# The third product of the mixers' output projection in whole float32, in a decoder block on one Trainium2 core

## The chip, the cores and the metric

The kernel runs on one core of a Trainium2 chip. The metric is the device time of one execution in microseconds; the median of the runs is quoted. Engines are named as in the profile: PE is TensorE's matmuls and PEld its weight loads, DVE is VectorE, ACT is ScalarE, POOL is GpSimd, SP is SyncE. SP and POOL issue most of the transfers from memory (DMAs).

## The reference

One decoder layer on 512 tokens of 1024 channels, with 256 memory tokens, all in float32. Three branches (a gated short convolution, a Conformer convolution, attention into the memory tokens) are weighted by gates and added; the sum goes through the output projection `w_o` (1024 x 1024), and the result is added to the residual rows. A gated feed-forward part and a norm follow.

```python
merged = g[:, :, 0] * y_a + g[:, :, 1] * y_b + g[:, :, 2] * y_c
x = x + merged @ w_o                                  # the product in question
h = _rmsnorm(x, norm_ffn_g)                           # needs every row of x
u = _causal_dwconv(h @ w_up, conv_ffn_w)
gt, up = jnp.split(u, 2, axis=-1)
x = x + (jax.nn.silu(gt) * up) @ w_down
return _rmsnorm(x, norm_final_g)
```

## The kernel before

**Products in parts.** PE multiplies in a reduced float32 form (`float32r`, fp32r in the profile). To keep the accuracy, each operand is split into a high part, a cast to that form, which ACT makes (`whi` or `whoh` of a weight, `mgh` of the merged activations), and a low part, the rest, which DVE makes (`wlo` or `whol`, `mgl`). One product is then three matmuls: high by high, high by low, low by high (`product`, L429 to L431). For some weights the low part is made by a DMA that adds the weight to the negated high part (L499, on POOL's queue).

**Seven products for eight.** A large product is cut into 2 x 2 blocks and worked out as seven block products by sums and differences of blocks (Strassen's scheme). In the output projection they are called a, b, f, c, d, e, g, in this order (`WO = "abfcdeg"`); f is the third. Each has an activation operand of 128 x 1024 (the blocks `m00`, `m01`, `m10`, `m11`, tiles `mg`, changed in place by L435 and L1627 between the products), a weight operand in two halves (tiles `wo`, sums of blocks of `w_o` made by DVE in L778 or by adding DMAs on POOL's queue in L1602 and L1609) and results of 2 x 128 x 512 in PSUM (`bank`). So each has 8 steps of 3 matmuls. f's weight is the tile `("wo", "x", i)`; c's and d's come from `("wo", "y", i)`, to which DVE adds f's weight for c and a POOL DMA adds another block for g; e has its own. DVE adds the results to the four row blocks of the residual, `x` (L1704).

**After the projection** ACT squares each row block (L1711) and takes the root (L1717), DVE scales it (L1722, `xnorm`), PE transposes it (L1730), and the products with `w_up` begin. The transposes of the first two row blocks stand ahead of each half of product g.

**The order of the work.** Nothing is issued when it is defined: `Jobs` collects all steps with an engine, a planned cost, what they need and which buffers they take. PE's steps keep the order in which they are written; for each other engine `Jobs.run` places the next step by planned start and due time, and gives out the buffers (the rings `sb` and `lf` in SBUF, `ps` in PSUM). Every engine and every DMA queue then works strictly in that order, so an instruction that waits holds up all behind it. The split weights take turns in four buffers, in the order of `the_unit`; six weight halves of the projection have buffers of their own (`WO_HELD`).

The casts of merged activations are written in L1644, their low parts in L1649; casts of weights in L478, their low parts in L482. ACT's cast of e's two weight halves needs the adding DMAs of L1602 to have landed.

Of the kernel before, what the change touches and what calls it, by code (L numbers as in the profile page):

```python
# [14 lines left out]
P = 128  # L15
# [39 lines left out]
HALF = SEQ // 2  # L55
LOAD_BUFS = 6
SHIFT = 192
SOON = 8.0

SHARE = 0.39  # L60
# [254 lines left out]
def hybrid_block_kernel(  # L315
# [19 lines left out]
    nc = tc.nc  # L335
# [29 lines left out]
    tiles = {}  # L365
# [14 lines left out]
    def two(key):  # L380

        return tiles[key].rearrange("p (c n) -> p c n", c=2)

    def four(key):
        return tiles[key].rearrange("p (k n) -> p k n", k=4)
# [14 lines left out]

    TAP = 0.665
    MM, MM_HALF, MM_QUAD = 0.2268, 0.12, 0.1142
    LOAD, MORE, MORE_WIDE = 1.42, 2.55, 2.55
    LOAD_LATENCY, MORE_LATENCY = 3.1, 3.4

# [36 lines left out]
    def pe(key, cost, fn, after=(), take=(), use=(), unit=True):  # L442
        pe_jobs[key] = (cost, fn, after, take, use)
        seq.append(key)
        if unit:
            the_unit(key, key)
# [8 lines left out]
    def split_job(unit, key, n_k, n, after, wide=None, lo_from=None, held=None):  # L455

        n_all = n_k * n

        def src():
            return wide() if wide is not None else tiles[key][:, :n_all]

        parts = []

        def high():
            if held:
                parts.extend(
                    forms.tile([P, 4, HALF], F32R, tag=held + s, name=name("who" + s)).rearrange(
                        "p k n -> p (k n)") for s in "hl"  # L470
                )
            else:
                parts.extend(
                    wts.tile([P, 1024], F32R, tag=s, name=name(s))[:, :n_all]
                    for s in ("whi", "wlo")
                )
            w_units[unit] = [t.rearrange("p (k n) -> p k n", k=n_k) for t in parts]
            nc.scalar.copy(parts[0], src())  # L478

        def low():  # L480
            hi, lo = parts
            nc.vector.tensor_tensor(lo, src(), hi.bitcast(F32), op=ALU.subtract)  # L482

        use = [key] if wide is None else []

        def define():
            if held:
                last = next(f for f in OPERAND if OPERAND[f] == held)
                before = [(("mq", 1), last)]
            else:  # L490
                i = unit_at[unit] - UNIT_BUFS
                before = [unit_uses[i][1]] if i >= 0 else []
            job(("wh", unit), "ACT", actv(n_all), high, list(after) + before, use=use)
            if lo_from is None:
                job(("wl", unit), "DVE", dve(n_all), low, [("wh", unit)], use=use)
            else:
                job(("wn", unit), "ACT", actv(n_all), lambda: nc.scalar.activation(
                    parts[1], src(), AF.Copy, scale=-1.0), [("wh", unit)], use=use)
                job(("wl", unit), "POOL", MORE, lambda: nc.gpsimd.dma_start(  # L499
                    out=parts[1], in_=lo_from, accum_op=ALU.add), [("wn", unit)],  # L500
                    MORE_LATENCY)

        deferred.append(define)
# [1079 lines left out]
    WO_SRC = {"a": (w_o[0, 0], w_o[0, 1]), "b": (w_o[0, 2], w_o[0, 3]), "d": (w_o[1, 2], w_o[1, 3])}  # L1583
    WO_LOWS = [(p, i) for p in "ab" for i in range(2)]

    def wo_bank(p):


        return "a" if p in "aceg" else "f" if p == "d" else p
# [4 lines left out]
    for i in range(2):  # L1594
        for key, src, take in (
            ("a", w_o[0, i], "wf"), ("b", w_o[0, 2 + i], "wf"), ("y", w_o[1, 2 + i], "lf"),
            ("x", w_o[0, i], "lf"), ("e", w_o[1, 2 + i], "sb"),
        ):
            after = {"y": late_rows, "x": late_rows, "e": [("wo", "a", 1)]}.get(key, ())
            fetch_job(("wo", key, i), src, after=after, take=(take,))  # L1600
        for key in "xe":
            job(("wadd", key, i), "POOL", MORE, lambda key=key, i=i: nc.gpsimd.dma_start(  # L1602
                out=tiles["wo", key, i], in_=w_o[1, i], accum_op=ALU.add),
                [("ld", ("wo", key, i))], MORE_LATENCY, use=[("wo", key, i)])
        deferred.append(lambda i=i: job(
            ("wsum", i), "DVE", dve(1024), lambda: add_into(("wo", "y", i), ("wo", "x", i)),
            [("wadd", "x", i), ("wl", ("wo", "d", i))], use=[("wo", "x", i), ("wo", "y", i)]))
        deferred.append(lambda i=i: job(
            ("wadd", "y", i), "POOL", MORE, lambda: nc.gpsimd.dma_start(  # L1609
                out=tiles["wo", "y", i], in_=w_o[0, 2 + i], accum_op=ALU.add),  # L1610
            [("wl", ("wo", "c", i))], MORE_LATENCY, use=[("wo", "y", i)]))
        for p, key, after in (
            ("a", "a", ("ld", ("wo", "a", i))), ("b", "b", ("ld", ("wo", "b", i))),
            ("d", "y", ("ld", ("wo", "y", i))), ("c", "y", ("wsum", i)),
            ("f", "x", ("wadd", "x", i)), ("e", "e", ("wadd", "e", i)),
            ("g", "y", ("wadd", "y", i)),
        ):
            split_job(("wo", p, i), ("wo", key, i), 2, 512, [after], held=WO_HELD.get((p, i)),
                      lo_from=WO_SRC[p][i] if (p, i) in WO_LOWS else None)

# [14 lines left out]
    def split_merged(n, p, at, halved, after):  # L1635
        src, hi, lo = SPLIT_FROM[p], ("mgh", p), ("mgl", p)
        first = not at.start
        end = (at.start // 512,) if halved else ()
        old = [hi + (0,)] if not first else []

        def high():
            if first:
                make(hi, F32R)
            nc.scalar.copy(tiles[hi][:, at], tiles[src][:, at])  # L1644

        def low():
            if first:
                make(lo, F32R)
            nc.vector.tensor_tensor(  # L1649
                tiles[lo][:, at], tiles[src][:, at], tiles[hi][:, at].bitcast(F32),  # L1650
                op=ALU.subtract
            )

        size = at.stop - at.start
        job(hi + end, "ACT", actv(size), high,
            after + old + ([wo_end(WO[n - 3])] if n > 2 else []),
            take=[(hi, "sb")] if first else [], use=[src] + ([] if first else [hi]))
        job(lo + end, "DVE", dve(size), low, [hi + end] + ([lo + (0,)] if not first else []),
            take=[(lo, "sb")] if first else [], use=[src, hi] + ([] if first else [lo]))

    for n, p in enumerate(WO):
        if p in "ab":
            m = 0 if p == "a" else 2
            for i in range(2):
                split_merged(n, p, slice(512 * i, 512 * (i + 1)), True, [("sum", 1, m + i, 0)])
        else:
            split_merged(n, p, slice(0, 1024), False,
                         [("sum", 1, 3, 1)] if p == "g" else [("ms", p)])

    def wo_lows(p, i):  # L1670
        return ("mgl", p, i) if p in "ab" else ("mgl", p)

    def wo_product(p, i, ts):
        w_hi, w_lo = w_units[("wo", p, i)]
        for k in (2 * i, 2 * i + 1):
            for t in ts:
                bank = ("bank", "wo", wo_bank(p), t)
                ps = make(bank) if p not in WO_BEFORE and k == 0 else tiles[bank]
                at = (slice(None), k, slice(t * P, (t + 1) * P))
                product(  # L1680
                    ps, w_hi[:, k % 2, :], w_lo[:, k % 2, :], four(("mgh", p))[at],
                    four(("mgl", p))[at], p not in WO_BEFORE and k == 0, k == 3, again=p in WO_BEFORE,
                )

    def pe_wo(p, i):

        before = WO_BEFORE.get(p)
        for ts in ((0, 1),) if p in "ab" else ((0,), (1,)):
            banks = [("bank", "wo", wo_bank(p), t) for t in ts]
            needs = [("wl", ("wo", p, i)), wo_lows(p, i)]  # L1690
            if i == 0 and before:
                needs += [("x1", before, t) for t in ts]
            new = p not in WO_BEFORE and i == 0
            key = ("wo", p, i) if len(ts) == 2 else ("wo", p, i, ts[0])
            pe(key, 6 * len(ts) * MM, lambda ts=ts: wo_product(p, i, ts), needs,
               take=[(b, "ps") for b in banks] if new else [],
               use=[("mgh", p), ("mgl", p)] + ([] if new else banks), unit=False)
        if (p, i) not in WO_HELD:
            the_unit(("wo", p, i), key)

    def add_row(p, t):
# [591 lines left out]
```

## Time and profile before

| | |
|---|---|
| time, median of 3 runs (lowest to highest) | 935.26 us (935.26 to 935.38) |
| span of the profiled execution | 933.7 us |
| median less that span | 1.56 us |
| PE busy | 916.0 us, 98% |
| DVE busy | 851.4 us, 91% |
| ACT busy | 689.5 us, 74% |
| POOL busy | 137.1 us, 15% |
| DMA traffic | 196.91 MB, mean 211 GB/s |
| chain that ended last | PE 86%, DVE 5%, ACT 5%, DMA 2% |

The page gives the profiled execution's own time as its span, from the first instruction to the last; what lies around it is in the runs' times only. A row of a timeline has the start, the length, the engine, the line, the instruction, output<-inputs and, in brackets, how long the engine was idle before it and what it waited for. Matmuls overlap: the time that one adds is the distance to the next start, not its length. The output projection runs from 558 to 606 us of the span.

### The profile page before, as it was taken

Reading aid. Unit: us, or ns where it says so; the run is one execution under the profiler, and the core shown is the slowest. Engines: PE = TensorE matmul, PEld = TensorE weight load, DVE = VectorE, ACT = ScalarE, POOL = GpSimd, SP = SyncE. Lnnn points to the kernel's source line nnn. Section 1 sums busy time; section 2 is a strip of 40 time slices with the busy share of each in tenths; the row PEclk is TensorE's granted clock in tenths of the full one; section 3 lists DMA queues with packets and bytes.
Section 4 is the critical chain, followed back from the end, with each engine's and each line's share of the span. In section 5 each row is a group of like instructions: output and inputs, shape, how many; then the busy total and the mean of one; then the engine's idle time right before and its main releaser. Section 6 shows DMA issues by size and latency. Waiting matters only on the chain.

```text
span 933.7 us, 17138 instructions
## 1 busy us (share of the span) xinstructions
PE 916.0 (98%) x6821; PEld 866.9 (93%) x6821; DVE 851.4 (91%) x979; ACT 689.5 (74%) x941; POOL 137.1 (15%) x165
## 2 busy tenths in 40 slices
PE   9999999999999999999999998999999999999996
PEld 8999999999889999999899896799999999988885
DVE  6898999999989999999886899897999889999986
ACT  8578988889978877878667983675766666765665
POOL 0121111100011111120100211111221111002300
PEclk9999999999999999999999998999999999999999
DMA  9999679745688998888868899799999886689952
GB/s 361 380 246 221 134 181 207 178 114 113 165 185 220 205 204 195 225 181 209 181 142 217 198 268 302 188 224 300 279 241 233 204 163 131 163 308 318 251 112 90
DMA packets 55952, 196.91 MB, mean 211 GB/s; under 512 B 6336, under 2 KB 6464, under 8 KB 55872
## 3 DMA queue, kind: packets, MB, share of 16 engines
q0 software_dynamic: 22608, 81.54, 48.8%
q1 hardware_dynamic: 32544, 113.23, 34.0%
q8 instruction: 53, 0.87, 0.4%
q10 hardware_dynamic: 720, 1.06, 0.3%
q14 instruction: 27, 0.22, 0.1%
HBM read 191.60 MB, written 4.19 MB: 210 GB/s over the span
## 4 chain that ended last, share of the span: by engine, by line
PE 86%; DVE 5%; ACT 5%; DMA 2%; issue 1%; SPq 0%; ACTq 0%; DVEq 0%
PE bank L659 56%; PE bank L431 6%; PE bank L429 6%; PE bank L430 6%; PE bank L1465 3%; PE bank L1464 3%; PE bank L1466 3%; PE bank L915 2%; DVE wlo L482 2%; ACT whi L478 1%; DMA wf<-in_w_up 1%; ACT acc L1322 1%; DMA wf<-in_w_v 1%; DVE mg L1539 0%; PE ss L788 0%
## 5 line engine op out<-in xcount | busy, mean ns | idle before, releaser
L478 ACT CAST whi<-wf 128x1024 fp32r<-128x1024 f32 x202 | 210.7, 1045 | 92.0 <-PE bank L659 39.9
L482 DVE TENSOR_TENSOR wlo<-wf,whi 128x1024 fp32r<-128x1024 f32 (+1 forms) x196 | 235.9, 1210 | 23.4 <-ACT whi L478 23.1
L1224 ACT ACTIVATE tp<-u,pk 128x510 f32<-128x510 f32 (+22 forms) x184 | 119.0, 705 | 4.4 <-DVE acc L1231 2.0
L1231 DVE TENSOR_TENSOR acc<-acc,tp 128x988 f32<-128x988 f32 (+22 forms) x92 | 109.1, 1187 | 8.8 <-ACT tp L1224 7.4
L616 POOL DMA_DIRECT2D wf<-in_w_in x48 | 42.5, 922 | 232.7 <-DVE wlo L482 165.3
L659 PE MATMUL bank<-fb10h,whi 128*128 128x256 f32 x248 | 69.0, 278 | 1.7 <-ACT g L709 1.2
L659 PE MATMUL bank<-fb10l,whi 128*128 128x256 f32 x248 | 68.7, 277 | 0.6 <-DVE fb10l L1369 0.6
L659 PE MATMUL bank<-ft6h,whi 128*128 128x256 f32 x248 | 68.8, 278 | 0.2 <-ACT gt L686 0.2
L659 PE MATMUL bank<-fb11h,wlo 128*128 128x256 f32 x248 | 68.6, 277 | 0.3 <-DVE wlo L482 0.3
L659 PE MATMUL bank<-fb00h,whi 128*128 128x256 f32 x248 | 68.8, 277 | 0.0
L659 PE MATMUL bank<-ft7h,whi 128*128 128x256 f32 x248 | 68.7, 277 | 0.0
L659 PE MATMUL bank<-ft7l,whi 128*128 128x256 f32 x248 | 68.7, 277 | 0.0
L659 PE MATMUL bank<-ft7h,wlo 128*128 128x256 f32 x248 | 68.7, 277 | 0.0
L659 PE MATMUL bank<-fb00l,whi 128*128 128x256 f32 x248 | 68.7, 277 | 0.0
L659 PE MATMUL bank<-ft6l,whi 128*128 128x256 f32 x248 | 68.7, 277 | 0.0
L659 PE MATMUL bank<-fb00h,wlo 128*128 128x256 f32 x248 | 68.7, 277 | 0.0
L659 PE MATMUL bank<-ft6h,wlo 128*128 128x256 f32 x248 | 68.7, 277 | 0.0
L659 PE MATMUL bank<-ft5h,wlo 128*128 128x256 f32 x248 | 68.7, 277 | 0.0
L659 PE MATMUL bank<-ft5h,whi 128*128 128x256 f32 x248 | 68.7, 277 | 0.0
L659 PE MATMUL bank<-ft5l,whi 128*128 128x256 f32 x248 | 68.7, 277 | 0.0
L659 PE MATMUL bank<-fb11h,whi 128*128 128x256 f32 x248 | 68.7, 277 | 0.0
L659 PE MATMUL bank<-fb10h,wlo 128*128 128x256 f32 x248 | 68.6, 277 | 0.0
(414 smaller groups left out, 3165.0 us busy)
## 6 DMA issues: line engine op xcount, KB each, us to landing
wf<-in_w_in SPq DMA_DIRECT2D x52, 512.0 KB, 5.5
wf<-in_w_in POOLq DMA_DIRECT2D x48, 512.0 KB, 6.7
wf<-in_w_up POOLq DMA_DIRECT2D x31, 512.0 KB, 7.2
wf<-in_w_up SPq DMA_DIRECT2D x29, 512.0 KB, 7.0
wf<-in_w_down SPq DMA_DIRECT2D x15, 512.0 KB, 4.6
wf<-in_w_att_out SPq DMA_DIRECT2D x8, 512.0 KB, 3.9
wf<-in_w_a_out SPq DMA_DIRECT2D x8, 512.0 KB, 4.5
wf<-in_w_b_out SPq DMA_DIRECT2D x8, 512.0 KB, 5.8
```

What stands on the lines that cost most here:

```text
L429: nc.tensor.matmul(ps, s_hi, w_hi, start=start, stop=False, skip_group_check=again)
L430: nc.tensor.matmul(ps, s_hi, w_lo, start=False, stop=False, skip_group_check=again)
L431: nc.tensor.matmul(ps, s_lo, w_hi, start=False, stop=stop, skip_group_check=again)
L478: nc.scalar.copy(parts[0], src())
L482: nc.vector.tensor_tensor(lo, src(), hi.bitcast(F32), op=ALU.subtract)
L616: nc.gpsimd.dma_start(out=tiles[key], in_=block(w, col[c], k), accum_op=ALU.add)
L659: nc.tensor.matmul(ps[:, c, :], w[:, k, at], a[k], start=first and n == 0, stop=i == 3 and n == 2, skip_group_check=again,)
L1224: nc.scalar.activation(two(("tp", p, s))[:, j, s:], two(("u", p))[:, j, : SEQ - s], AF.Copy, scale=weight(j),)
L1231: nc.vector.tensor_tensor(a, a, two(("tp", p, s))[:, :, s:], op=ALU.add)
L1464: nc.tensor.matmul(ps, w_hi[:, i, at], hi, start=first, stop=False)
L1465: nc.tensor.matmul(ps, w_hi[:, i, at], lo, start=False, stop=False)
L1466: nc.tensor.matmul(ps, w_lo[:, i, at], hi, start=False, stop=last)
```

## The change

Product f takes its operands as they are, in whole float32: the merged block and the two weight halves are neither cast nor split, and each of its 8 steps is one matmul. Its weight buffers, and those of the split activation, are no longer taken, and the planner counts 0.87 per matmul in place of three times 0.2268. The planner places the other engines' steps anew from these numbers; on PE all other matmuls stand in the same order as before. The diff, cut where nothing is changed in what f does:

```diff
+WO_WHOLE = "f"
...
+    MM_WHOLE = 0.87
...
+            if p in WO_WHOLE:
+                whole[p, i] = (("wo", key, i), after)
+                continue
             split_job(("wo", p, i), ("wo", key, i), 2, 512, [after], held=WO_HELD.get((p, i)),
                       lo_from=WO_SRC[p][i] if (p, i) in WO_LOWS else None)
...
+    def merged(p):
+        return [("sum", 1, 1, 1), ("sum", 1, 3, 1)] if p == "g" else [("ms", p)]
...
-        else:
-            split_merged(n, p, slice(0, 1024), False,
-                         [("sum", 1, 3, 1)] if p == "g" else [("ms", p)])
+        elif p not in WO_WHOLE:
+            split_merged(n, p, slice(0, 1024), False, merged(p))
...
+    def wo_whole(p, i, ts):
+        w, m = two(whole[p, i][0]), four(SPLIT_FROM[p])
+        for k in (2 * i, 2 * i + 1):
+            for t in ts:
+                bank = ("bank", "wo", wo_bank(p), t)
+                first = p not in WO_BEFORE and k == 0
+                nc.tensor.matmul(
+                    make(bank) if first else tiles[bank], m[:, k, t * P : (t + 1) * P],
+                    w[:, k % 2, :], start=first, stop=k == 3, skip_group_check=p in WO_BEFORE,
+                )
...
-            needs = [("wl", ("wo", p, i)), wo_lows(p, i)]
+            if p in WO_WHOLE:
+                work, cost, needs = wo_whole, 2 * MM_WHOLE, [whole[p, i][1]] + merged(p)
+                parts = [SPLIT_FROM[p], whole[p, i][0]]
+            else:
+                work, cost, needs = wo_product, 6 * MM, [("wl", ("wo", p, i)), wo_lows(p, i)]
+                parts = [("mgh", p), ("mgl", p)]
...
-            pe(key, 6 * len(ts) * MM, lambda ts=ts: wo_product(p, i, ts), needs,
+            pe(key, cost * len(ts), lambda ts=ts: work(p, i, ts), needs,
...
-        if (p, i) not in WO_HELD:
+        if (p, i) not in WO_HELD and p not in WO_WHOLE:
             the_unit(("wo", p, i), key)
```

More of the change, by code (lines that the diff above doesn't have):

```diff
@@ L1584, in hybrid_block_kernel @@
     WO_LOWS = [(p, i) for p in "ab" for i in range(2)]
+    whole = {}
     def wo_bank(p):
@@ L1694, in pe_wo @@
             key = ("wo", p, i) if len(ts) == 2 else ("wo", p, i, ts[0])
-            pe(key, 6 * len(ts) * MM, lambda ts=ts: wo_product(p, i, ts), needs,
+            pe(key, cost * len(ts), lambda ts=ts: work(p, i, ts), needs,
                take=[(b, "ps") for b in banks] if new else [],
-               use=[("mgh", p), ("mgl", p)] + ([] if new else banks), unit=False)
-        if (p, i) not in WO_HELD:
+               use=parts + ([] if new else banks), unit=False)
+        if (p, i) not in WO_HELD and p not in WO_WHOLE:
             the_unit(("wo", p, i), key)
```

## The prediction

> **What bounds the kernel now.** I read the page's head and its chain, then the waits of TensorE (PE), then the timeline of the stretch with the longest wait, and last the rows of the engines that feed it. Line numbers are those of the kernel before.
>
> ```profile
> span 933.7 us, 17138 instructions
> PE 916.0 (98%) x6821; PEld 866.9 (93%) x6821; DVE 851.4 (91%) x979; ACT 689.5 (74%) x941; POOL 137.1 (15%) x165
> PE bank L431 <- DVE mgl L1649: 3.3, 1, 3.3
> PE bank L429 <- DVE x L1704: 0.8, 1, 0.8
> ```
>
> The first two lines are the page's, the next two come from PE's waits (line, releaser, us in total, times, longest). PE is busy 98% of the span, so a microsecond is won where PE stands or runs slowly. The longest wait, 3.3 us, lies in the third product (f) of the output projection, the one that is changed. Its timeline (start, length, instruction, idle time before it) and three stretches of the windows view (stretch, length, busy time of PE, PEld, DVE, ACT, POOL; granted clock, DMA share, GB/s):
>
> ```profile
> 569.25 0.48 PE L429 MATMUL bank<-whi,mgh 128*128 128x512 f32 x1
> 569.58 0.40 PE L430 MATMUL bank<-wlo,mgh 128*128 128x512 f32 x1
> 573.29 0.79 PE L431 MATMUL bank<-whi,mgl 128*128 128x512 f32 x1 [3.32 <-DVE mgl L1649]
> 573.89 0.63 PE L429 MATMUL bank<-whi,mgh 128*128 128x512 f32 x1
> 578.58 0.52 PE L431 MATMUL bank<-whi,mgl 128*128 128x512 f32 x1
> 578.94 0.40 PE L429 MATMUL bank<-whi,mgh 128*128 128x512 f32 x1
> 581.02 0.39 PE L429 MATMUL bank<-whi,mgh 128*128 128x512 f32 x1
> 569.90:573.30 3.40, 0.08 (x2) 0.01 (x1) 3.40 (x4) 1.28 (x2) 2.64 (x3) 0.81 1.01 320
> 573.30:578.60 5.30, 5.30 (x13) 4.14 (x14) 5.30 (x6) 2.09 (x2) 0.00 (x0) 0.50 1.05 299
> 586.40:592.00 5.60, 5.60 (x25) 4.50 (x25) 4.28 (x5) 1.48 (x2) 0.61 (x1) 1.00 1.05 231
> ```
>
> Product f runs from 569.25 to 581.02, where product c begins: 11.77 us for 24 matmuls. The nine that start from 578.94 on take (581.02 - 578.94) / 9 = 0.231 us each, so 24 would take 5.55 us. The surplus of 6.2 us has two parts: PE stands 3.3 us, and then the granted clock is 0.50, so that thirteen matmuls take 578.94 - 573.29 = 5.65 us in place of 3.0, which is 2.65 us. Why the low part mgl comes late, VectorE (DVE) shows; it has no gap here:
>
> ```profile
> 552.66 1.22 DVE L482 TENSOR_TENSOR wlo<-wo,whi 128x1024 fp32r<-128x1024 f32 x1
> 554.99 1.22 DVE L482 TENSOR_TENSOR wlo<-wo,whi 128x1024 fp32r<-128x1024 f32 x1
> 566.88 1.22 DVE L1627 TENSOR_TENSOR mg<-mg,mg 128x1024 f32<-128x1024 f32 x1
> 568.02 0.68 DVE L1704 TENSOR_TENSOR x<-x,bank 128x512 f32<-128x512 f32 x1
> 568.62 1.22 DVE L482 TENSOR_TENSOR wlo<-wo,whi 128x1024 fp32r<-128x1024 f32 x1
> 572.02 2.35 DVE L1649 TENSOR_TENSOR mgl<-mg,mgh 128x1024 fp32r<-128x1024 f32 x2
> ```
>
> The operand of f, the subtraction of L1627, is there at 568.1, before PE wants it at 569.25. Only its low part, behind three other instructions, comes at 573.2.
>
> **The change, part by part.** *Removed work.* DVE loses three instructions: the two wlo of f (552.66 and 554.99) and its mgl. ScalarE (ACT) loses their three casts. Here is DVE before, from the weight sum ahead of f's subtraction on; wo_6182 is the first half of f's weight, wo_6233 that of d's, c's and g's in turn, wo_6640 the second half of the same, mg the merged activations, x the residual rows, bank the results in PSUM.
>
> ```order
> L778 TENSOR_TENSOR wo_6233<-wo_6233,wo_6182 128x1024
> L1627 TENSOR_TENSOR mg_6643<-mg_6645,mg_6643 128x1024
> L1704 TENSOR_TENSOR x_836_6520<-x_836_6520,bank_6602 128x512
> L482 TENSOR_TENSOR wlo_6668<-wo_6233,whi_6667 128x1024
> L435 SCALAR_TENSOR_TENSOR mg_6482<-mg_6643,mg_6482 128x1024
> L482 TENSOR_TENSOR whol_6691<-wo_6640,whoh_6690 128x1024
> L1649 TENSOR_TENSOR mgl_6700<-mg_6643,mgh_6673 128x1024
> L1649 TENSOR_TENSOR mgl_6702<-mg_6482,mgh_6698 128x1024
> ```
>
> DVE in the changed kernel, from f's subtraction to c's first wlo:
>
> ```order
> L1635 TENSOR_TENSOR mg_6619<-mg_6635,mg_6619 128x1024
> L1730 TENSOR_TENSOR x_835_6519<-x_835_6519,bank_6600 128x512
> L438 SCALAR_TENSOR_TENSOR mg_6482<-mg_6619,mg_6482 128x1024
> L781 TENSOR_TENSOR wo_6233<-wo_6233,wo_6182 128x1024
> L1730 TENSOR_TENSOR x_843_6563<-x_843_6563,bank_6604 128x512
> L1657 TENSOR_TENSOR mgl_6669<-mg_6482,mgh_6661 128x1024
> L485 TENSOR_TENSOR wlo_6667<-wo_6233,whi_6666 128x1024
> ```
>
> f's subtraction now stands ahead of the weight sum, and two wlo further up are gone. An instruction of 1024 columns takes 568.02 - 566.88 = 1.14 us from start to start, so the subtraction ends 3 x 1.14 = 3.4 us earlier, near 564.6. Behind it, to the end of c's wlo, stand six instructions: two of 0.6 us (x, 568.02 to 568.62) and four of 1.14 us, 5.8 us, so c's wlo ends at 570.4, against 569.8 before. f then waits for nothing (4.6 us in hand), and c, with both low parts there at 570.4, has 6 us in hand.
>
> *Added work.* On PE eight float32 matmuls of 512 columns stand in f's place, between the same neighbours. The trace has none such. The nearest is the warm-up, nine of 128 columns, and each leaves two records:
>
> ```profile
> 1.36 4.19 PE L1841 MATMUL bank<-ident 128*128 128x128 f32 x18 [1.36 <-POOL ident masks.py:199]
> L1841 PEld LDWEIGHTS bank<-ident x18: 286/333/333, 1.4 to 4.9; 128*128 128x128 f32 x18
> L429 PEld LDWEIGHTS bank<-whi,mgh x32: 186/188/333, 569.2 to 605.0; 128*128 128x128 f32 x32
> ```
>
> They take 4.19 / 9 = 0.466 us each, and their weight loads last 333 ns, as the longest of the L429 group does and not as its median of 188: PE then ran at about half speed. At full speed that is 0.233 us, and for four times the columns 0.93 us: the upper end. The lower end is two records as long as those of f, 2 x 0.231 = 0.46 us. I take 0.93 us, since the warm-up is the row of the same kind: 8 x 0.93 = 7.4 us (lower end 3.7), 1.9 us more than 5.55. [...]
>
> So f runs from 569.25 to 576.7, and c starts 4.3 us sooner than at 581.02. At the lower end c could start sooner still, but what follows then holds it.
>
> *What is late next.* c, d and e follow, 4.3 us earlier. e's two weights are read and then added to by DMAs on POOL's queue, and these stand behind the add that waits for c's wlo:
>
> ```profile
> 570.13 0.86 POOL L1609 DMA_DIRECT2D wo<-in_w_o  x1 [11.04 <-DVE wlo L482]
> 570.66 2.11 POOL L1602 DMA_DIRECT2D wo<-in_w_o  x2
> DMA to landing us min/median/max: 12.8/14.5/16.1
> 587.42 1.05 ACT L478 CAST whi<-wo 128x1024 fp32r<-128x1024 f32 x1 [1.34 <-DMA wo<-in_w_o]
> 591.58 1.06 ACT L1711 ACTIVATE xnorm<-x 128x1024 f32<-128x1024 f32 x1 [3.10 <-DVE x L1704]
> 593.03 1.06 ACT L1711 ACTIVATE xnorm<-x 128x1024 f32<-128x1024 f32 x1 [0.30 <-ACT xnorm L1711]
> 594.20 1.28 ACT L1717 ACT_TABLE_LOAD   x1
> 596.02 1.28 DVE L1722 SCALAR_TENSOR_TENSOR xnorm<-x,cols,gffn 128x1024 f32<-128x1024 f32 x1
> 597.52 1.03 PE L1730 MATMUL bank<-ident,xnorm 128*128 128x128 f32 x8
> 599.35 0.50 PE L429 MATMUL bank<-whi,mgh 128*128 128x512 f32 x1 [0.80 <-DVE x L1704]
> ```
>
> The third row is the time from issue to landing of L1602's two adds: the second is issued at 571.2 and lands 16.1 us later, at 587.3. ACT's cast of e's second half waits for it until 587.42. With c's wlo 0.6 us later POOL issues 0.5 us later, and it lands at 587.8. Behind that cast, on ACT, stand the squares of the first two rows (L1711). Before, they waited until 591.58 for the results of d. Shifted by 4.3 us these would be there at 587.3, but ACT is in its cast from 587.9 to 588.95. The two squares take 594.20 - 591.58 - 0.30 = 2.3 us, so the table load comes at 591.3, not 594.20: 2.9 us earlier. xnorm, the transposes and the last product g keep their distances behind it: xnorm at 593.1, g at 596.45. But PE is done with e at 597.52 - 4.3 = 593.2, and stands about 1.3 us until xnorm is written and some 0.9 ahead of g. Thus 1.4 of the 4.3 us go back.
>
> *A load that moves.* SP's rows keep their order, but other buffers are given out. SP before, with the semaphores each load waits for; x_847 is the third block of rows, wo_6663 and wo_6670 are e's weights:
>
> ```order
> L1557 DMA x_842_6558<-in_x 128x1024 [waits DMAHW4_49]
> L1557 DMA x_847_6600<-in_x 128x1024 [waits DMAHW5_49]
> L508 DMA wo_6640<-in_w_o 128x1024 [waits DVE_49]
> L508 DMA wo_6663<-in_w_o 128x1024 [waits DMAHW7_49,PE_49]
> L508 DMA wo_6670<-in_w_o 128x1024 [waits DMAHW0_49,Activation_49]
> ```
>
> SP in the changed kernel, the same five loads; e's weights are now wo_6658 and wo_6663:
>
> ```order
> L1560 DMA x_843_6563<-in_x 128x1024 [waits DMAHW4_49]
> L1560 DMA x_847_6615<-in_x 128x1024 [waits DMAHW5_49,DVE_49]
> L511 DMA wo_6639<-in_w_o 128x1024 [waits DVE_49]
> L511 DMA wo_6658<-in_w_o 128x1024 [waits DMAHW7_49,DVE_49]
> L511 DMA wo_6663<-in_w_o 128x1024 [waits DMAHW0_49,DVE_49]
> ```
>
> The third row block now waits for DVE, and e's loads no longer for PE. One load of 512 KB moves into a stretch where the DMA engines are full (share 1.05 in the window at 586.40). At that window's 231 GB/s it is at most 2.3 us of transfer, at least nothing, if the other loads' earlier start makes room. I take nothing for it, since POOL's adds have a queue of their own; the 2.3 us stay in the range.
>
> *Down the line.* From 600 us on PE waits little, so what is won at g is kept:
>
> ```profile
> PE bank L659 <- DVE wlo L482: 0.3, 1, 0.3
> PE bank L659 <- ACT gt L686: 0.2, 1, 0.2
> ```
>
> The sum: -4.3 + 1.4 = -2.9 us, span 930.8. The median of 935.26 lies 1.56 us above the span of 933.7; with the same around it the time is **932.4 us**.
>
> **The rivals.** *A: e's add does not bind.* If it lands before about 586.3, the whole 4.3 us stay: 931.0. For it: SP's loads go out earlier. Against it: POOL issues no earlier. 20%.
>
> *B: e's add lands late, and PE's clock falls.* The place is ACT's cast of e's second half. Each microsecond of landing after 587.8 costs one at the squares; with the full 2.3 us of the moved load it is 934.7, and at 590.7 the gain is gone. PE wants that half at 587.7 + 12 x 0.231 = 590.5 and gets it 2.2 us (cast and wlo) after the landing; from a landing at 591.5 on it has stood the 3.3 us after which the clock fell at 573.29, and another 2.65 us go: 932.4 + 3.7 + 2.65 = 938.7, slower than before. For it: both queues share full engines, and e's adds already took the longest to land. Against it: only one load's worth is added, 2.3 of the 3.7 us it takes. 14%; a landing between 588.8 and 591.5, 933.4 to 936.1, another 8%.
>
> *C: the clock falls at the new gaps* of 1.3 and 0.9 us; then 2.65 of the 2.9 us go: 935.0. The trace has a drop after 3.32 us and none after 0.80, so 1.3 lies nearer to none. [...] 7%.
>
> *D: the gain is lost again* in the stages after 600, where a DMA that cannot start sooner would be waited for: 935.3. PE's 0.5 us of waits there speak against it. 4%.
>
> **How the numbers follow.** The forecast itself has 47% (e's add landing within 1 us of 587.8: 931.4 to 933.4). A change under 0.2%, 1.9 us, can hardly be told from none. Faster: forecast and A, 0.67. Same: the landing between, C and D, 0.19. Slower: B, 0.14. The range goes from a little under A, where f's matmuls cost 0.06 us less each (931.0 - 8 x 0.06 = 930.5), to 936.1, the last landing before B; B alone lies beyond.
>
> **What would show it.** Right: no wait of PE at f, clock 1.00 from 569 to 587, eight float32 matmuls in 7.4 us, c at about 576.7; ACT waiting for the DMA of wo until 587.8, and PE waiting at the transposes. Wrong: f taking over 9 us, a wait at c, a second stretch at clock 0.50, the e add landing before 586 or after 590, or PE waiting after 600 for more than 1 us.

## The result, and the profile after

The changed kernel takes 932.02 us, the median of 10 runs (931.41 to 933.43); the kernel before, run beside it, takes 935.26 (933.22 to 937.50). The ratio is 0.9969, 95% interval 0.9960 to 0.9978: faster by about 3 us, in the range given, 0.4 us below the forecast of 932.4. The profiled execution took 931.92 us, its span is 930.2 us.

Product f starts at 568.46 us here and at 569.25 before. That offset is no gain of the change: PE's matmuls are 0.81 us sooner at 33 us already and stay so up to f, and in e9, the same program, they are 0.31 us sooner. Such offsets differ from one execution to the next (f starts between 568.4 and 571.1 us in the profiles below), so places in two profiles are compared by their distance from f's first matmul. Line numbers are higher by 3 in front of f's subtraction (L432 for L429, L485 for L482, L1607 for L1602) and by 26 behind (L1756 for L1730, L1730 for L1704, L1737 for L1711, L1743 for L1717); xnorm is L1748 for L1722.

TensorE's (PE's) waits around the projection (line, releaser, us in total, times, longest), then its timeline, both of the kernel after:

```profile
PE bank L1756 <- DVE cols L1747: 1.0, 1, 1.0
PE bank L432 <- DVE x L1730: 0.8, 1, 0.8
```

```profile
568.46 7.03 PE L1701 MATMUL bank<-wo,mg 128*128 128x512 f32 x16
574.92 0.80 PE L432 MATMUL bank<-whi,mgh 128*128 128x512 f32 x1
575.56 0.40 PE L433 MATMUL bank<-wlo,mgh 128*128 128x512 f32 x1
593.06 1.06 PE L1756 MATMUL bank<-ident,xnorm 128*128 128x128 f32 x8 [1.03 <-DVE cols L1747]
594.96 0.67 PE L432 MATMUL bank<-whi,mgh 128*128 128x512 f32 x1 [0.84 <-DVE x L1730]
599.42 1.04 PE L1756 MATMUL bank<-ident,xnorm 128*128 128x128 f32 x8
```

The wait of 3.3 us at f is gone. f's eight matmuls, two records each, take 7.03 us. The first matmul of c overlaps f's last and is 0.64 us ahead of its second, where 0.23 is usual; counted back from the second, c begins at 575.33, 6.9 us behind f's start, against 11.77 before. Two new gaps stand around the first transposes: 1.03 us ahead of them, 0.84 us ahead of g. Now what feeds them, from the timelines of VectorE (DVE), POOL and ScalarE (ACT):

```profile
562.80 1.23 DVE L1635 TENSOR_TENSOR mg<-mg,mg 128x1024 f32<-128x1024 f32 x1
568.54 1.22 DVE L485 TENSOR_TENSOR wlo<-wo,whi 128x1024 fp32r<-128x1024 f32 x1
570.59 2.11 POOL L1607 DMA_DIRECT2D wo<-in_w_o  x2
586.66 1.05 ACT L481 CAST whi<-wo 128x1024 fp32r<-128x1024 f32 x1 [2.84 <-PE bank L434]
587.62 1.05 ACT L1737 ACTIVATE xnorm<-x 128x1024 f32<-128x1024 f32 x1
588.66 1.04 ACT L1737 ACTIVATE xnorm<-x 128x1024 f32<-128x1024 f32 x1
589.81 1.28 ACT L1743 ACT_TABLE_LOAD   x1
591.63 1.28 DVE L1748 SCALAR_TENSOR_TENSOR xnorm<-x,cols,gffn 128x1024 f32<-128x1024 f32 x1
```

The time from issue to landing of the two adds into e's weights (the row at 570.59), least, median and most:

```profile
DMA to landing us min/median/max: 12.1/13.8/15.5
```

ACT stands 2.84 us until 586.66, where it casts e's second half of weights. The second add into it was issued at 571.1 and landed 15.5 us later, at 586.6: the cast waits for that, although the view names PE. In a second profile of the same program (e9 below) the view names the transfer for the same cast:

```profile
586.87 1.05 ACT L481 CAST whi<-wo 128x1024 fp32r<-128x1024 f32 x1 [2.61 <-DMA wo<-in_w_o]
```

In both profiles the squares follow the cast with no gap, then the table load, the roots and xnorm, and behind xnorm the transposes.

The windows view after the first gap (stretch, length, busy time of PE, PEld, DVE, ACT, POOL; granted clock, DMA share, GB/s) shows what the forecast did not have:

```profile
591.72:595.13 3.41, 1.54 (x11) 1.02 (x10) 3.37 (x5) 3.41 (x5) 0.00 (x0) 1.00 1.04 269
595.13:598.55 3.42, 3.42 (x9) 2.65 (x10) 3.42 (x4) 1.22 (x3) 0.00 (x0) 0.50 0.06 12
598.55:601.96 3.41, 3.41 (x21) 2.90 (x20) 2.19 (x3) 2.34 (x4) 0.86 (x1) 1.00 0.74 183
```

For 3.41 us, in g's first half, the clock is 0.50. So in this execution the second transposes come 30.96 us behind f's start (33.00 before), a gain of 2.0 us there.

### The profile page after: what moved, and what is told of

Read it like the earlier page. It is cut to its first block, busy times and chain, and to the rows that moved or that the text cites. A ratio compares the mean times of both kernels' runs of the same rounds, so it can differ in the third digit from the quotient of the medians.

```text
span 930.2 us, 17118 instructions
## 1 busy us (share of the span) xinstructions
PE 915.1 (98%) x6813; PEld 863.5 (93%) x6813; DVE 848.1 (91%) x976; ACT 686.0 (74%) x938; POOL 137.4 (15%) x165
## 4 chain that ended last, share of the span: by engine, by line
PE 83%; issue 7%; DMA 4%; DVE 3%; ACT 1%; POOL 1%; ACTq 0%; POOLq 0%; DVEq 0%
PE bank L662 55%; PE bank L432 6%; PE bank L434 6%; PE bank L433 5%; PE bank L1469 3%; PE bank L1467 3%; PE bank L1468 3%; PE bank L918 2%; DMA wo<-in_w_o 2%; DMA wf<-in_w_b_out 2%; DMA wf<-in_w_up 1%; DVE wlo L485 1%; ACT whi L481 0%; PE bank L1155 0%; POOL whol L502 0%
## 5 line engine op out<-in xcount | busy, mean ns | idle before, releaser
L485 DVE TENSOR_TENSOR wlo<-wf,whi 128x1024 fp32r<-128x1024 f32 (+1 forms) x196 | 235.8, 1210 | 23.5 <-ACT whi L481 23.2
L662 PE MATMUL bank<-fb11l,whi 128*128 128x256 f32 x248 | 68.5, 276 | 0.0
```

What stands on the lines that cost most here:

```text
L662: nc.tensor.matmul(ps[:, c, :], w[:, k, at], a[k], start=first and n == 0, stop=i == 3 and n == 2, skip_group_check=again,)
```

## The experiments

Three questions: how much of the gain is the wait and how much the clock behind it; whether e's landing holds the transposes now; what the clock at the two new gaps costs. Each ratio is to the kernel before, run beside it (median 935.20 for e1 to e4, 934.76 for e5 to e8, 934.53 for e9 to e12).

**e1: f in split form, its low part earlier.** The kernel before, one due time changed:

```diff
-"DVE ms c": -4,
+"DVE ms c": -4, "DVE mgl f": -4,
```

> The kernel before, with f still in its three-pass split form; the low part of f's merged sums is moved to stand right behind c's low weights on VectorE, ahead of d's. Theory (what the change gained is the wait of 3.3 us ahead of f's last matmuls and the half clock behind it, 2.65 us; the matmuls themselves cost about the same in both forms): TensorE's wait at f falls to 1.5 us or less, the clock stays at 1.00 from 569 to 593 us, c starts about as early as in the changed kernel, and the time is 931 to 933.5 us, within 1 us of the changed kernel's 932.0. Rival (the gain comes from the operations that the change takes off VectorE and ScalarE, or from the whole float32 matmuls): those are all still there, and the time stays at 934.5 to 936.

Measured: 933.35 us, ratio 0.9980 (0.9971 to 0.9989). PE's waits, then two stretches of the windows view:

```profile
PE bank L1730 <- DVE xnorm L1722: 2.2, 2, 2.0
PE bank L431 <- DVE mgl L1649: 1.0, 1, 1.0
```

```profile
596.05:599.47 3.42, 1.41 (x7) 0.81 (x6) 3.38 (x5) 2.50 (x5) 0.86 (x1) 1.00 0.79 273
599.47:602.88 3.41, 3.41 (x13) 3.02 (x14) 2.60 (x4) 2.07 (x4) 0.86 (x1) 0.50 0.78 139
```

The wait at f is 1.0 us and the clock holds there. c begins 6.93 us behind f's start (569.42 to 576.35), as early as in the changed kernel (6.87). With no work taken from DVE or ACT and no whole float32 anywhere, 1.9 of 3.2 us are won, so the rival falls. The time is in the theory's range, but 1.3 us above the changed kernel, where it had expected 1 at most. What is missing goes at the second transposes: the planner, with new due times, put the second xnorm behind other work on DVE, and PE waits 2.0 us, with a half clock behind it.

**e5: the wait filled with other work.** The kernel before, with small matmuls ahead of f's first:

```diff
+                if (p, k, t) == ("f", 0, 0):
+                    for _ in range(10):
+                        nc.tensor.matmul(ps[:, :P], ident, ident, start=True, stop=True)
```

> The kernel before with ten small float32 matmuls of 128 columns (the identity by itself, about 0.23 us each) put into f's own bank right ahead of f's first matmul, so that TensorE works through most of its wait there; their result is overwritten and nothing else is moved. Theory (of the 4.3 us that the change wins ahead of c, 2.65 us are the half clock behind the wait and not the wait): TensorE's wait at f falls to about 1.1 us and ends at the same place as before, the clock stays at 1.00 from 573 to 579 us, c starts 2.6 us sooner than before, and the time is 932.4 to 933.4 us against the 935.2 of before. Rival 1 (what the clock costs there is given back behind, where e's weights or another landing sets the end): the clock stays at 1.00 and the time is 934.5 to 935.5. Rival 2 (a wait of 1.1 us is enough for the clock to fall): no change.

Measured: 933.16 us, ratio 0.9983 (0.9974 to 0.9993). PE's timeline, then the stretch with the wait in the windows view:

```profile
569.34 2.39 PE L1682 MATMUL bank<-ident 128*128 128x128 f32 x20
571.49 0.48 PE L429 MATMUL bank<-whi,mgh 128*128 128x512 f32 x1
573.38 0.50 PE L431 MATMUL bank<-whi,mgl 128*128 128x512 f32 x1 [1.18 <-DVE mgl L1649]
595.04 1.03 PE L1733 MATMUL bank<-ident,xnorm 128*128 128x128 f32 x8
```

```profile
571.79:575.21 3.42, 2.24 (x10) 1.51 (x9) 3.42 (x5) 0.34 (x1) 1.06 (x2) 1.00 0.92 327
```

f's third matmul starts no sooner than before (4.04 us behind the place where f began, as before), the clock stays, and the first transposes come 25.70 us behind that place where it was 28.27: 2.6 us, the 2.65 of the half clock. In the time 1.6 us of it are seen. That is half of what the change wins, from the clock alone; rivals 1 and 2 fall.

The runs of the kernel before agree. Of the 77 that stand beside the experiments, 67 have a mean clock of 0.996 or less and a median of 934.8 us; the six with 0.998 took 932.2 to 932.7. None of the six has a profile, but 0.998 leaves no room for the half clock behind f's wait: 3.41 us of it lower the mean of such a span by 0.0018, and the half clock at the very end, behind the last matmul, by another 0.0015 to 0.0033 in the profiles here.

**e2: half of f.** The changed kernel, f one step of k shorter in each half:

```diff
-        for k in (2 * i, 2 * i + 1):
+        for k in (2 * i,) if i == 0 else (2 * i + 1,):
```

> The changed kernel with four of f's eight whole float32 matmuls left out (half of f's sum is not computed). Theory (behind f, it is the landing of e's second half of weights and not TensorE's own work that sets when g starts): f is 3.5 us shorter, c, d and e start 3.5 us sooner, TensorE's gaps ahead of the transposes and of g grow from 1.0 and 0.8 us, g starts within 1 us of 595, and the time is 931.0 to 934 us (above 932 if the longer gaps cost more of the clock). Rival (TensorE's work is what counts): everything is 3.5 us sooner, and the time is 928 to 929.5.

Measured: 931.57 us, ratio 0.9967 (0.9954 to 0.9979), as the changed kernel: 3.5 us less work on PE buy nothing that can be told. PE's timeline:

```profile
569.26 3.60 PE L1701 MATMUL bank<-wo,mg 128*128 128x512 f32 x8
576.75 0.50 PE L433 MATMUL bank<-wlo,mgh 128*128 128x512 f32 x1 [0.75 <-DVE wlo L485]
586.62 0.50 PE L433 MATMUL bank<-wlo,mgh 128*128 128x512 f32 x1 [1.25 <-DVE wlo L485]
593.50 1.06 PE L1756 MATMUL bank<-ident,xnorm 128*128 128x128 f32 x8 [1.25 <-DVE cols L1747]
```

PE waits in c and in e for low parts of weights, and again at the transposes, which start 24.2 us behind f's start against 24.6. So something other than PE's own work sets when they start.

**e4: e's adds left out.**

```diff
-lambda key=key, i=i: nc.gpsimd.dma_start(
+lambda key=key, i=i: key == "x" and nc.gpsimd.dma_start(
```

> The changed kernel without the two adding transfers of GpSimd into e's weights (the second part of e's weight sum is left out), so that these weights are there some 15 us sooner. Theory (the squares on ScalarE, and with them the gaps around the first transposes, wait behind the cast of e's second half, which waits for its landing at 586.6 us): both casts are done before d's rows are, the squares start at about 585.9 and 586.8, right behind those rows, the table load is 1.4 us or more earlier, the gap ahead of the transposes shrinks to below 0.3 us, and the time is 929 to 930.8. Rival (the landing doesn't bind, d's rows or TensorE's own work do): the squares start at 587.6 as now, and the time stays at 931.5 to 932.5.

Measured: 930.52 us, ratio 0.9950 (0.9938 to 0.9963). ACT's and PE's timelines:

```profile
586.46 1.06 ACT L1737 ACTIVATE xnorm<-x 128x1024 f32<-128x1024 f32 x1 [2.75 <-issue]
588.67 1.28 ACT L1743 ACT_TABLE_LOAD   x1
591.93 1.06 PE L1756 MATMUL bank<-ident,xnorm 128*128 128x128 f32 x8
593.83 0.49 PE L432 MATMUL bank<-whi,mgh 128*128 128x512 f32 x1 [0.83 <-DVE x L1730]
```

The squares start 1.16 us sooner than in the changed kernel, f having started at the same time (568.44); the view names nothing, and DVE is done with d's rows at 586.4. The gap ahead of the transposes is gone, and the time falls by 1.1 to 1.5 us (against 931.62 in e9 and 932.02). With e2 this settles the point: in the changed kernel e's landing holds the squares, and through them g.

**e3 and e10: the gap ahead of the transposes filled.** The changed kernel, twice:

```diff
-            make(("bank", "tr", t, i))
+            ps = make(("bank", "tr", t, i))
+            if (t, i) == (0, 0):
+                for _ in range(4):
+                    nc.tensor.matmul(ps[:, :P], ident, ident, start=True, stop=True)
```

> The changed kernel with four small float32 matmuls of 128 columns (the identity by itself) put into the first transposes' own bank right ahead of them; their result is overwritten, nothing else is moved. Theory (the half clock from 595 to 599 us, in which g's first 12 matmuls took 0.43 us each in place of 0.23, follows from the gaps of 1.0 and 0.8 us ahead of and behind the first transposes): with the first gap filled the clock stays at 1.00 there, g's first block is 1.5 to 2.4 us shorter, and the time is 929.8 to 931. Rival 1 (the fall has another cause, or the gap behind the transposes is enough by itself): the clock falls as before and the time stays at 931.5 to 932.5. Rival 2 (the block is given back behind 600 us): the clock stays at 1.00 and the time is 931.5 to 932.5.

> The same edit as in the third run (four small matmuls ahead of the first transposes in the changed kernel), beside the changed kernel on one chip. Theory (the gaps around the transposes cost the clock in some executions only): 0.3 to 1.0 us below the changed kernel. Rival (they cost it nearly always): 1.4 to 2.2 us below. Rival 2 (nothing there reaches the end): within 0.3 us of it.

Measured: 931.62 us, ratio 0.9964 (0.9952 to 0.9977), and 931.55, ratio 0.9973 (0.9962 to 0.9984). **e9** is the changed kernel beside e10:

> The changed kernel again, unaltered, so that the next three stand beside it on the same chip. Every theory expects 0.2 to 0.4 per cent below the kernel before, 931.5 to 932.8 us. It also shows how the time of one execution goes with its mean clock: if the half clock behind the first transposes comes and goes, executions with a mean clock of 0.996 should be 1 to 2 us above those with 0.998 or more.

Measured: 931.62 us (930.75 to 933.71), ratio 0.9967 (0.9957 to 0.9977). So the filling buys nothing that can be told; e10's rival 2 holds, and the theories of e3 and e10 fall. The profile of e9 tells why, PE's timeline first and then the windows view:

```profile
593.28 1.06 PE L1756 MATMUL bank<-ident,xnorm 128*128 128x128 f32 x8 [0.80 <-DVE cols L1747]
595.18 0.50 PE L432 MATMUL bank<-whi,mgh 128*128 128x512 f32 x1 [0.84 <-DVE x L1730]
598.06 1.04 PE L1756 MATMUL bank<-ident,xnorm 128*128 128x128 f32 x8
```

```profile
592.44:595.85 3.41, 1.78 (x12) 1.44 (x12) 3.37 (x6) 3.41 (x6) 0.00 (x0) 1.00 1.00 250
595.85:599.27 3.42, 3.42 (x21) 2.90 (x20) 3.42 (x4) 1.73 (x4) 0.00 (x0) 1.00 0.24 26
```

The same program, a gap of 0.80 in place of 1.03 us, and the clock stays: g's first half takes 2.88 us, not 4.46. Of the changed kernel's 20 runs one has a mean clock of 0.996, and that is the one first profiled; the others have 0.997 to 0.999, and the profiles here without such a fall have 0.997 or 0.998. In that run, too, most was made good later: its second transposes come 1.84 us later behind f's start than those of e9 (30.96 against 29.12), the end of its span 0.7 (930.2 - 568.46 = 361.7 against 930.0 - 568.94 = 361.1).

**e6: g in whole float32 too**, and **e7: e too** (`WO_WHOLE = "fg"`, `"fe"`).

> The changed kernel with g, too, in whole float32 (its two casts of weights and its one of sums leave ScalarE, its three subtractions for low parts leave VectorE). Theory (a whole float32 product costs TensorE 7.0 us in place of 5.6 at full clock, and pays only where a wait goes; around g there is none of low parts): 1.0 to 2.0 us slower than the changed kernel, 932.8 to 934.0 us. Rival (the operations that leave VectorE and ScalarE pay by themselves, whatever waits): faster than the changed kernel, 930 to 931.5 us.

Measured: 933.08 us, ratio 0.9988 (0.9978 to 0.9997). PE's timeline, the first half of g:

```profile
595.65 3.70 PE L1701 MATMUL bank<-wo,mg 128*128 128x512 f32 x8 [0.84 <-DVE x L1730]
599.18 1.04 PE L1756 MATMUL bank<-ident,xnorm 128*128 128x128 f32 x8
```

3.53 us where e9 has 2.88: 0.65 a half, 1.3 for g, and the time is 1.1 to 1.5 us above the changed kernel's, as the theory had it. Six operations less on DVE and ACT do not pay for it. Whole float32 was dearer for PE here, by this 0.65 us a half; only at f did it remove a wait.

> The changed kernel with e, too, in whole float32. ScalarE then has no cast of e's weights ahead of the squares; on GpSimd's queue e's two adding transfers then stand behind both of g's. Theory (the cast of e's second half, which waits for its landing, is what holds the squares): the squares start at about 586 and 587 us, the table load 1.2 us or more sooner; TensorE's e is 1.4 us longer, so that the gap ahead of the first transposes is gone and the clock stays at 1.00 there; 931.0 to 932.3 us. Rival (e's adds now land too late for TensorE itself, after 590 us): a new wait of 1 to 4 us ahead of e's second half, and 932.8 to 935 us.

Measured: 936.96 us, ratio 1.0023 (1.0013 to 1.0033), outside both. The gap ahead of the transposes is gone, but DVE's new order put two low parts of weights ahead of d's rows, and the squares start no sooner (589.07, 19.6 us behind f's start; 18.9 in e9). Later PE waits 1.1 us for a low part and 2.4 us for ACT's copy of a gate, with a half clock behind the latter (657.07 to 660.48 us), in up products whose feeding steps the planner had also moved. As a test of e's landing it says nothing.

**e8: e's adds ahead of g's** on POOL's queue. Of the diff one line is shown; the others let these adds be placed up to 100 us ahead instead of 10 and give the cast and the low part of g's second half due times of their own.

```diff
-"POOL wadd e": 5.82,
+"POOL wadd e": -20,
```

> The changed kernel with the two adding transfers into e's weights issued ahead of the one into g's first half on GpSimd's queue, in place of behind it (and g's first cast on ScalarE behind e's casts, its second at its old place by a rule of its own); nothing is left out. Theory (e's second half then lands at 575 to 583 us, and the squares start right behind d's rows, as they do where e's adds are left out): the gap ahead of the first transposes is below 0.5 us, the clock stays at 1.00 to 600 us, and the time is 930.3 to 931.5 us. Rival (g's first half now lands late, at 583 to 588 us, and its cast holds the squares in the same way): the squares start at 587 us or later and the time is 931.7 to 933 us.

Measured: 933.52 us, ratio 0.9988 (0.9978 to 0.9998). The timelines of POOL and ACT:

```profile
571.01 0.86 POOL L1607 DMA_DIRECT2D wo<-in_w_o  x1 [10.50 <-DMA wo<-in_w_o]
587.63 1.05 ACT L481 CAST whi<-wo 128x1024 fp32r<-128x1024 f32 x1 [1.82 <-DMA wo<-in_w_o]
590.61 1.06 ACT L1737 ACTIVATE xnorm<-x 128x1024 f32<-128x1024 f32 x1 [1.94 <-DVE x L1730]
```

The rival's case, by one engine more; the time is above its range too. e's adds cannot go before e's loads have landed, at 571, and hold the queue until then. g's first half now lands at 587.6; its low part stands ahead of d's rows on DVE, and these hold the squares (19.5 us behind f's start, 18.9 in e9).

**e11: the square root's table loaded early.** The changed kernel, one instruction more, in the cast of weights:

```diff
             nc.scalar.copy(parts[0], src())
+            if unit == ("wo", "e", 0):
+                nc.scalar.activation(column(10, 1), eps, AF.Sqrt)
```

> The changed kernel with one square root of a constant column on ScalarE right behind the cast of e's first half, where that engine stood idle for 2.8 us, so that the table of the square root is loaded there and not between the squares and the roots; nothing is left out. Theory (squares, table load and roots on ScalarE hold the first transposes, the gap ahead of them being 1.0 us): no table load behind the squares, the scaled rows 1.3 us sooner, the gap ahead of the transposes below 0.2 us, the clock at 1.00 to 600 us, and the time 1.0 to 2.2 us below the changed kernel, 929.8 to 931.3 us. Rival (TensorE's own work or e's landing is what holds them, and what is won is waited for again): within 0.4 us of the changed kernel.

Measured: 930.04 us (929.74 to 930.82), ratio 0.9952 (0.9939 to 0.9965), in the theory's range and 1.6 us below e9. This version beats both kernels. The timelines of ACT and PE:

```profile
584.67 1.28 ACT L483 ACT_TABLE_LOAD   x1
590.15 0.47 ACT L1745 ACTIVATE cols<-cols,eps 128x1 f32<-128x1 f32 x2
592.40 1.03 PE L1758 MATMUL bank<-ident,xnorm 128*128 128x128 f32 x8
594.00 0.50 PE L432 MATMUL bank<-whi,mgh 128*128 128x512 f32 x1 [0.57 <-DVE x L1732]
596.86 1.03 PE L1758 MATMUL bank<-ident,xnorm 128*128 128x128 f32 x8
```

The load lies where ACT waited for e's landing. The roots follow the squares, the gap ahead of the transposes is gone, and the second transposes come 27.85 us behind f's start (29.12 in e9).

**e12: the same in the kernel before.**

> The kernel before with the same early square root behind the cast of e's first half. Theory (before the change TensorE itself was late there, with no gap ahead of the first transposes, so that this chain on ScalarE cost nothing; only the change laid it bare): within 0.4 us of the kernel before, 934.5 to 935.6 us. Rival (the chain always held something): 1.0 to 1.5 us below, 933.5 to 934 us.

Measured: 933.36 us (930.66 to 936.67), ratio 0.9989 (0.9977 to 1.0001): 1.2 us below the kernel before, which is the rival's distance, but with an interval that takes in no change at all. PE's row behind its wait at f, then the windows view there:

```profile
572.93 0.50 PE L431 MATMUL bank<-whi,mgl 128*128 128x512 f32 x1 [3.31 <-DVE mgl L1651]
570.06:573.47 3.41, 0.54 (x2) 0.49 (x3) 3.41 (x4) 1.04 (x1) 2.36 (x3) 1.00 0.90 324
573.47:576.88 3.41, 3.41 (x9) 2.65 (x8) 3.41 (x5) 1.04 (x1) 0.00 (x0) 0.50 1.00 284
```

PE still waits 3.3 us at f, but only 3.41 us of half clock follow, not 6.83 as in the profile before. The 0.8 us ahead of g are gone: e's rows, whose bank g takes, stand behind both xnorms on DVE, and these come sooner. So in the profile before this chain did cost PE 0.8 us, and the theory's "nothing" does not fit; the time neither shows nor excludes it.

## Why the prediction was right, and where it was not

- *f's wait and the half clock go, c 4.3 us sooner.* Right; it is 4.9 (11.77 less 6.87). The term of f's matmuls was 0.6 too high: by the distance to c's start they take 0.86 us each (6.87 / 8), not 0.93. The upper end was the one to take: of the 3.7 us at the lower end nothing is seen. The warm-up did run at half speed: in e5, at clock 1.00, ten such matmuls lie 2.15 us ahead of f's first (569.34 to 571.49), 0.215 each, and four times that is the 0.86 measured at f. The 0.6 us did not reach the time, because e's landing holds what follows.
- *The half clock, 2.65 us, as a sure part of the gain.* Its size was right for the profiled execution (2.6 in e5), but it is not fixed. By the mean clock 67 of 77 runs have it; 40 of these, at 0.996, have room for one window of 3.41 us only (median 934.6 us), as e12's profile shows, and 27 have less (935.2). In the time it is worth 1.6 us by e5 and 2.3 by the runs that lack it.
- *f's surplus of 6.2 us has two parts.* The parts named, 3.3 and 2.65, make 5.95. The other 0.26 lies around the wait too: from f's first matmul to its third are 4.04 us (573.29 less 569.25), 3.32 of them the wait and 0.46 two matmuls at 0.231. It goes with the wait, so the 4.3 us stand.
- *c has 6 us in hand; the moved load costs nothing.* As foretold: no wait at c. c's wlo ends 1.3 us behind f's start (568.54 + 1.22 less 568.46), forecast 1.2 (570.4 less 569.25). e's second half is cast 18.2 us behind f's start (17.9 in e9), forecast 18.55. The load itself was not tested apart.
- *e's landing holds the squares, and part of what is won goes back.* Right in kind, by e2 and e4, which speak against rival A. The term was too large: the table load is 3.6 us sooner behind f's start (3.9 in e9), not 2.9, because the landing came 0.4 to 0.6 us sooner and cast, squares and table load stand closer than I had added them up. The gaps were 1.03 and 0.84 us (0.80 and 0.84), forecast 1.3 and 0.9.
- *What is won at g is kept.* Nearly: in e9 the second transposes are 3.9 us sooner behind f's start, the end of the span 3.4 (361.1 against 364.5 us). In the first profile, with the clock's loss, they are 2.0 sooner and the end 2.7 (361.7). So up to 0.7 us move behind 600 us, which no step of mine had. Most of it is no wait: from 608 to 636 us PE is busy throughout at clock 1.00 in all three profiles, yet gets through 247 matmuls in the first one and 241 in e9 and before. Why they lie closer there is open.
- *Rival B*, the late landing: did not come. *Rival C*, the clock at the new gaps: I had judged each gap by itself, 1.3 us lying nearer to 0.80 than to 3.32. That step was wrong: the falls in these profiles go with the idle time of both together, 1.87 us in one window of 3.41 where the clock fell, 1.63 in e9 where it did not (the last section). The clock did fall in the first profile, behind two gaps of 1.03 and 0.84 us, and a second stretch at 0.50 was one of my signs of being wrong; but by the mean clock that is 1 run of 20, and its time, 931.92, lies with the others.

That 932.02 lies so near 932.4 is in part luck: about 1 us more was won at g than forecast, and half of it was lost again behind 600 us (e9).

## What to carry to other kernels

Price a wait of TensorE in two parts, the wait and the clock behind it: here filling the wait with idle work saved the second alone (e5, 1.6 of 3.2 us). When a wait goes, follow the chain that is late next to its engine and look for something on it that needs no input, as the table load here, which one early instruction took off the path (1.6 us more). An edit that lets a planner place everything anew must be judged by the whole profile: e1, e7 and e8 each lost elsewhere some or all of what they should have won.

## What the hardware showed that I had not expected

In the profiles of this case the granted clock changed on a grid of 3.41 us, and its falls went with PE's idle time within one such window, not with the longest gap: it fell behind gaps of 1.03 and 0.84 us (the changed kernel) and not behind one of 1.25 (e2, at 586.62). Between any two changes of the granted clock in a profile lay a whole number of windows of 3.413 us: in the kernel before 2 from 572.01 to 578.84 us, and 103 more to the fall at 930.41, behind the last matmul. So the places of change lay the grid of a profile; in e9, where the clock holds to the end, its fall at 926.94 does, 97 windows behind 595.85. The windows view of the kernel before, on its grid:

```profile
568.60:572.01 3.41, 1.37 (x6) 0.63 (x4) 3.41 (x4) 2.54 (x3) 1.88 (x3) 1.00 1.03 375
572.01:575.43 3.42, 2.13 (x5) 1.75 (x6) 3.42 (x5) 0.04 (x1) 0.76 (x1) 0.50 1.01 316
575.43:578.84 3.41, 3.41 (x9) 2.64 (x9) 3.41 (x4) 2.09 (x2) 0.00 (x0) 0.50 1.05 271
```

The window with 2.04 us idle (3.41 less 1.37) is followed by one at half clock; that one, with 1.28 us idle, by another; behind this, which has none idle, the clock is 1.00 again, from 578.84. Other falls were seen behind windows with 1.87 (the changed kernel), 2.01 (e1) and 2.87 us idle (e12), none behind 1.63 (e9) or 1.18 (e5). Laid over the fourteen profiles from their first to their last change of clock, the grid had no exception: every full-clock window with 1.87 us idle or more was followed by half clock, none with less. The largest without a fall is one of e6, behind which the clock is still full:

```profile
920.93:924.34 3.41, 1.62 (x14) 1.42 (x12) 2.39 (x8) 1.85 (x5) 0.00 (x0) 1.00 0.38 149
```

So in these profiles the least idle time with a fall behind it is 1.87 us of 3.41, the most without one 1.79 (3.41 less 1.62). Nearly the same gaps stood at the transposes in the two profiles of the changed kernel: 1.03 and 0.84 us put 1.87 us of idle time into one window, and the clock fell; 0.80 and 0.84 put 1.63 there, and it did not. That the idle time of the window is the cause is my reading of these rows; no run changed it alone.

A table load took 1.28 us in every row shown here, and in e11 the casts and squares between the early load and the roots needed no other.
